# A position-bias table written from 128 partitions in three pieces, and the first loads of inverse blocks issued by ScalarE, in a hybrid DeltaNet and dilated-attention layer

## Chip, cores and metric

One NeuronCore of a Trainium2 chip runs the whole layer. Times are device microseconds of one execution. The reported time of a kernel is the median of several executions; one further execution is taken with a profile, and all rows shown come from that one.

## The reference

One sequence of 2048 tokens with model width 1024, all in float32. Cut to what matters here:

```python
proj = rms_norm(x, norm_w) @ w_in                  # 2048 x 4104
# branch 1: gated delta rule, 4 heads of 128, chunks of 64 tokens
l_mat = a_mat + eye                                # per chunk, lower triangular 64 x 64
u = triangular_solve(l_mat, v * beta);  w = triangular_solve(l_mat, k * beta * exp(gc))
def step(state, (a, q_dec, k_tail, u, w, g_last)): # over the 32 chunks, in order
    v_new = u - w @ state
    o     = q_dec @ state + a @ v_new
    state = state * g_last + k_tail.T @ v_new
y_dn = rms_norm(o) * silu(z)
# branch 2: 8 heads of 64, three dilated windows (128,1), (512,4), (2048,16)
scores = q @ k.T + rel_bias[:, t5_bucket(distance)]   # one bias table per head and pattern
o = softmax-weighted sum of the three patterns, * silu(gate)
out = x + concat(y_dn, o) @ w_out
```

## The kernel before

The work runs in stages, and TensorE is kept filled by mixing a projection (its products go to the PSUM tiles `pj`) with whatever else is due. A scheduler with priorities sets the order of instructions on each engine ahead of time; on the chip each engine runs its list strictly in order.

- **Convolution and inverses** (to about 440 us). The projections of q, k and v of the delta rule are convolved. `stage1a` builds the chunk matrices and stores them to DRAM (`A_d`, `Es_d`); `inverse(hf)` inverts their 32 x 32 diagonal blocks on VectorE and stores them (`A_d`, `D0_d`), first for chunks 0 to 15 (hf 0), then for 16 to 31. Hf 0 is stored at about 370 us and hf 1 at about 440 us.
- **Gate projection** (L187 to L208, `gate_proj`). Its second half, over token blocks 0 and 1, runs from about 444 us, with 24 products a block: TensorE fills a `pj` tile (two of them), VectorE multiplies it into a tile `t` (two of them), ScalarE applies SiLU and issues the store to `gate`.
- **The bias table** (L577 to L590). `rel_bias` (32 x 8) and a one-hot matrix (33 x 768) are loaded into the tile `K` (named `scr` in the code), their product (8 heads x 768 columns) is copied back into `K`, and three transfers write it to DRAM as `bs_d`, each pattern's row of 256 numbers 64 times per head. The attention stage reads the table back with a stride of 255, which gives each query its shifted row. The first such read is at 644 us.
- **Delta rule** (about 450 to 800 us). `stage2(pair, c0)` prepares four chunks of two heads: it loads `kT`, `qT`, `vT`, `Qr`, `E`, `TT` (the inverse blocks, tiles `TTz`) and `D0` (tiles `D0t`), completes the 64 x 64 inverses on TensorE (first step: `A<-D0t,TTz`, L637 before, L642 after) and makes the operands of `chain(pair, c, g)`, the step from chunk to chunk. `dn_out(pair, c0, g)` normalises four chunks, multiplies them by `zs` (loaded there) and stores them to `y_d`. Beside all this the attention's projection (`pj`, 128x256, line L99) fills TensorE.
- **Attention and output projection** (about 800 us to the end).

All loads before the change, and most stores, are issued from SyncE's queue (SP), in order; ScalarE (ACT) issues some stores. Both share eight completion counters, which the tables below call DMAHW0 to DMAHW7 (the number behind the underscore says nothing here). Each transfer takes the next counter, and is issued only when the last transfer that used that counter has landed. So at most eight transfers of the two queues are under way, and an issue can wait for a transfer it has nothing to do with.

Of the kernel before, what the change touches and what calls it, by code (L numbers as in the profile page):

```python
# [8 lines left out]
F32 = mybir.dt.float32  # L9
# [7 lines left out]
P = 128  # L17
S = 2048
# [6 lines left out]
NOSYNC = mybir.DependencyInfo(mybir.DependencyClass.NoSync, mybir.DependencyReason.DATA)  # L25
CH = 64
# [15 lines left out]
N_BUCKETS = 32  # L42
# [38 lines left out]
def dap(t, off, dims):  # L81
    return bass.AP(tensor=t.tensor, offset=t.offset + off, ap=[list(d) for d in dims])


def hybrid(tc, xT, x, norm_w, w_in, conv_w, a_log, dt_bias, dn_norm_w, q_norm_w, k_norm_w,
# [23 lines left out]
    nc = tc.nc  # L109
# [13 lines left out]
    dma = nc.sync.dma_start  # L123
    adma = nc.scalar.dma_start

    dr, _ = pool("dr", space=DRAM)
    qkvT_d = [[dr.tile([P, 32, 2, CH], F32, name=f"cv{w}{p}") for p in range(2)] for w in range(3)]
    zs_d = dr.tile([S, 512], F32, name="zs_d")
    gate_d = [dr.tile([P, S], F32, name=f"gate{p}") for p in range(4)]
    rows_d = dr.tile([4, 4, S], F32, name="rows_d")  # L130
    rstd_d = dr.tile([1, S], F32, name="rstd_d")

    A_d = [dr.tile([2, 16, P, CH], F32, name=f"A{i}") for i in range(2)]
    Es_d = [dr.tile([2, 16, P, CH], F32, name=f"Es{i}") for i in range(2)]
    D0_d = [dr.tile([64, 32, 32], F32, name=f"D0{i}") for i in range(2)]
    qkT_d = [[dr.tile([P, S], F32, name=f"qk{w}{p}") for p in range(4)] for w in range(2)]
    v_d = dr.tile([S, 512], F32, name="v_d")
    y_d = dr.tile([S, 512], F32, name="y_d")
    bs_d = dr.tile([8, 3, 64 * 256], F32, name="bs_d")
    ml_d = [[dr.tile([2, 96, CH], F32, name=f"ml{h}{p}") for p in range(4)] for h in range(2)]  # L140
    F_d = [[dr.tile([3, 2, 1024], F32, name=f"F{h}{p}") for p in range(4)] for h in range(2)]
    mx_d = dr.tile([4, P, S], F32, name="mx_d")
# [76 lines left out]
    nc = engines  # L219
    dma = nc.sync.dma_start  # L220
    adma = nc.scalar.dma_start
# [100 lines left out]
    for kt in range(KT):  # L322
# [14 lines left out]
        for i in range(4):  # L337
            for j, (x_, w_) in enumerate(((xh, 0), (xh, 1), (xl, 0))):
                nc.tensor.matmul(pz[i][:, :260], x_[0][:, kt, i * P:(i + 1) * P], wz[0][kt][w_][:, kt % 4, :260],
                                 start=kt == 0 and j == 0, stop=kt == KT - 1 and j == 2)  # L340
# [3 lines left out]
    n = KT  # L344
# [35 lines left out]
    nc = tc.nc  # L380
    dma = nc.sync.dma_start
    adma = nc.scalar.dma_start
# [12 lines left out]
    at = ba[:, 4:8, :]  # L395
# [180 lines left out]
    scr = at0.tile([P, S], F32, name="K0")  # L576
    rb = scr[:N_BUCKETS + 1, 1536:1544]  # L577
    nc.vector.memset(rb, 1.0)
    dma(scr[:N_BUCKETS, 1536:1544], rel_bias)
    oh = scr[:N_BUCKETS + 1, 768:1536]  # L580
    dma(oh, onehot)
    bv = scr[:8, :768].rearrange("p (a b) -> p a b", a=3)
    for i in range(2):
        pb = psA.tile([P, 512], F32, name="pm", bufs=1)
        n = 512 - 256 * i
        nc.tensor.matmul(pb[:8, :n], rb, oh[:, i * 512:i * 512 + n], start=True, stop=True)
        nc.vector.tensor_copy(scr[:8, i * 512:i * 512 + n], pb[:8, :n])
    for i in range(3):
        dma(dap(bs_d, i * 64 * 256, [[3 * 64 * 256, 8], [256, 64], [1, 256]]),
            bv[:, i, None, :].to_broadcast([8, 64, 256]))  # L590

# [4 lines left out]
    turn2 = [0]  # L598
    SU = psD.tile([P, 4, P], F32, name="SU", bufs=1)

    def stage2(pair, c0):

        hf, cc = divmod(c0, 16)
        u0 = pair * 32 + c0
        m0 = pair * 32 + cc * 2
# [7 lines left out]
        dma(vT, qkvT_d[2][pair][:, c0:c0 + 4])  # L615
        Qr = dn.tile([P, 4, 2, CH], F32, name="Qr", bufs=1)
        for s_ in range(2):
            dma(Qr[:, :, s_], dap(rows_d, (12 + 2 * pair + s_) * S + c0 * CH, [[0, P], [CH, 4], [1, CH]]))
        WQ = dn.tile([P, 4, 2, P], F32, name="WQ", bufs=3)
        for s_ in range(2):  # L620
            nc.gpsimd.tensor_tensor(WQ[:, :, s_, (1 - s_) * CH:(2 - s_) * CH], Qr[:, :, s_], qT[:, :, 1 - s_],
                                    op=ALU.mult)
        E = dn.tile([P, 4, CH], F32, name="E2", bufs=2)
        dma(E, Es_d[hf][pair, cc:cc + 4].rearrange("u p i -> p u i"))
        TT = TTz[n2 % 2]
        D0 = dn.tile([P, 4, 32], F32, name="D0t", bufs=2)
        Xs = dn.tile([P, 4, 32], F32, name="Xs", bufs=1)
        for s_ in range(2):
            a = s_ * CH
            dma(TT[a:a + CH, :, a:a + CH], A_d[hf][pair, cc:cc + 4, a:a + CH].rearrange("u p i -> p u i"))  # L630
            dma(D0[a:a + 32], dap(D0_d[hf], (m0 + s_) * 1024, [[32, 32], [2048, 4], [1, 32]]))
        pa = psD.tile([P, 512], F32, name="A", bufs=2)
        px, pn = pa[:, :256].rearrange("p (a u i) -> p a u i", a=2, u=4), pa[:, 256:260]
        for u in range(4):
            for s_ in range(2):
                a, b = s_ * CH, s_ * CH + 32
                nc.tensor.matmul(px[b:b + 32, 0, u], TT[a:a + 32, u, b:b + 32], D0[a:a + 32, u], start=True, stop=True)  # L637
        for s_ in range(2):
            b = s_ * CH + 32
            nc.vector.tensor_copy(Xs[b:b + 32], px[b:b + 32, 0])  # L640
        for u in range(4):
            for s_ in range(2):  # L642
                a, b = s_ * CH, s_ * CH + 32
                nc.tensor.matmul(px[a:a + 32, 1, u], Xs[b:b + 32, u], TT[b:b + 32, u, b:b + 32], start=True, stop=True)
        for s_ in range(2):
            a = s_ * CH
# [4 lines left out]
        for u in range(4):  # L651
            nc.tensor.matmul(pq[:, u], kT[:, u].rearrange("p s i -> p (s i)"), qT[:, u].rearrange("p s i -> p (s i)"),
                             start=True, stop=True)
        for u in range(4):
            nc.tensor.matmul(pn[:, u:u + 1], q2[:, u], one, start=True, stop=True)
        at_ = dn.tile([P, 4, P], F32, name="at_", bufs=3)
        nc.gpsimd.memset(at_[:CH, :, :CH], 0.0)  # L657
        nc.gpsimd.memset(at_[CH:, :, CH:], 0.0)
        for s_ in range(2):
            a, b = slice(s_ * CH, (s_ + 1) * CH), slice((1 - s_) * CH, (2 - s_) * CH)  # L660
# [6 lines left out]
        Ks = dn.tile([P, 4, 2, P], F32, name="Ks", bufs=3)  # L667
# [27 lines left out]
        U = dn.tile([P, 4, P], F32, name="U", bufs=3)  # L695
        nc.scalar.copy(U, pu)
        o4 = dn.tile([P, 4, P], F32, name="o4", bufs=2)
        return dict(WQ=WQ, at=at_, Ks=Ks, U=U, o4=o4)

    Sst = []  # L700
    mark = {}
# [34 lines left out]
    def dn_out(pair, c0, g):  # L736
        u0 = pair * 32 + c0
        zs = dn.tile([P, 4, P], F32, name="zs", bufs=1)
        for s_ in range(2):
            h = 2 * pair + s_  # L740
            dma(zs[(1 - s_) * CH:(2 - s_) * CH], dap(zs_d, c0 * CH * 512 + h * P, [[512, CH], [CH * 512, 4], [1, P]]))
        f = dn.tile([P, 2, 4], F32, name="f", bufs=2)
        nc.vector.tensor_scalar(f[:, 0], ssqq[:, u0:u0 + 4], EPS, EPS * P, op0=ALU.add, op1=ALU.mult)
        nc.vector.scalar_tensor_tensor(f[:, 1], ssqo[:, u0:u0 + 4], 1.0 / P, f[:, 0], op0=ALU.mult, op1=ALU.add)
        nc.gpsimd.tensor_tensor(f[:, 1], f[:, 1], mhalf[:, :4], op=ALU.pow)
        for u in range(4):
            nc.vector.scalar_tensor_tensor(g["o4"][:, u], g["o4"][:, u], f[:, 1, u:u + 1], zs[:, u],
                                           op0=ALU.mult, op1=ALU.mult)
        for s_ in range(2):
            h = 2 * pair + s_  # L750
            dma(dap(y_d, c0 * CH * 512 + h * P, [[512, CH], [CH * 512, 4], [1, P]]),
                g["o4"][(1 - s_) * CH:(2 - s_) * CH])


    prio = {"chain": 1000000, "prep": PRPREP, "out": PROUT}

    def at_prio(k, f, *args):
        tc.cur_priority = prio[k]
        r = f(*args)
        prio[k] = tc.cur_priority  # L760
        return r

    G = {}
    for p_ in range(2):
        G[p_] = at_prio("prep", stage2, p_, 0)
    for c0 in range(0, 32, 4):
        cur = dict(G)
        for u in range(4):
            for p_ in range(2):
                at_prio("chain", chain, p_, c0 + u, cur[p_])  # L770
            if u == 0:
                for p_ in range(2):
                    if c0 + 4 < 32:
                        G[p_] = at_prio("prep", stage2, p_, c0 + 4)
        for p_ in range(2):
            at_prio("out", dn_out, p_, c0, cur[p_])
    close(psD_g)
    close(dn_g)

# [41 lines left out]
    nc = engines  # L821
# [140 lines left out]
    def heads(hf, p):  # L962
# [5 lines left out]
        def load():  # L968
            g["q1"] = at0.tile([P, 1024], F32, name="q1", bufs=QB)
            g["k1"] = KC[p % 2] if hf else K0[:, p % 2 * 1024:(p % 2 + 1) * 1024]  # L970
            dma(g["q1"], qkT_d[0][p][:, T0:T0 + 1024])
            dma(g["k1"], qkT_d[1][p][:, :1024 * (hf + 1)])
            g["bias"] = bias = at0.tile([P, 3, 192], F32, name="bias", bufs=2)
            for s_ in range(2):
                dma(bias[s_ * CH:(s_ + 1) * CH],
                    dap(bs_d, (2 * p + s_) * 3 * 64 * 256 + 63, [[255, CH], [64 * 256, 3], [1, 192]]))
            g["kc"] = {0: g["k1"].rearrange("p (c i) -> p c i", c=1)}

        def keys(pat):
# [259 lines left out]
    for i, g in enumerate(G):  # L1239
        b = 12 * i  # L1240
# [279 lines left out]
```

## Time and profile before

| | |
|---|---|
| median of three executions | 1446.1 us (1442.88 to 1447.8) |
| profiled execution | 1442.2 us, of which the span from first to last instruction is 1440.4 us |
| TensorE busy | 1374.0 us, 95% of the span |
| VectorE, ScalarE, GpSimd busy | 62%, 47%, 30% |
| mean granted TensorE clock | 0.987 |

TensorE is the engine to watch: it is busy nearly all the time, so what matters is where it stands still and where its clock is low. The granted clock is 1.00 (2.4 GHz) or 0.50 (1.2 GHz).

### The profile page before, as it was taken

To read this page: it belongs to the slowest core of one execution; us is meant where nothing else is said; L and a number is where in the kernel's file an instruction comes from. 1 tells how busy PE (TensorE), PEld (TensorE's weight loads), DVE (VectorE), ACT (ScalarE), POOL (GpSimd) and SP (SyncE) were. 2 spreads that over 40 slices of the span, in tenths; PEclk is the share of its full clock that TensorE was granted. 3 is DMA by queue.
4 is the path that set the end of the run, shared out by engine and by line. 5 is a ranking of instruction groups with operands and counts; after the bars stand their busy time and mean duration, and the time that the engine had idled before them with its cause. 6 is when DMAs were issued, how large, how long until landed. Compare 5 with 4: busy or idle time off the path is not lost.

```text
span 1440.4 us, 28745 instructions
## 1 busy us (share of the span) xinstructions
PE 1374.0 (95%) x10234; PEld 1223.6 (85%) x10234; DVE 897.2 (62%) x2786; ACT 680.1 (47%) x1937; POOL 427.2 (30%) x499
## 2 busy tenths in 40 slices
PE   7999999999998998999999899999998999999988
PEld 7998777777877887999999889999887778888877
DVE  6526678799894365777777554544354645466455
ACT  7634436642221333444444476665555545555520
POOL 0000000000002112442432523657466274655500
PEclk9999999999999999999999999999998999999999
DMA  7653445773557556566554554464448574755764
GB/s 218 165 117 70 99 102 133 156 132 55 116 88 193 147 83 171 133 166 168 133 143 76 124 127 116 100 174 119 112 118 246 146 247 134 216 154 171 200 175 150
DMA packets 301154, 205.00 MB, mean 142 GB/s; under 512 B 149283, under 2 KB 271027, under 8 KB 300500
## 3 DMA queue, kind: packets, MB, share of 16 engines
q1 hardware_dynamic: 233924, 171.70, 48.6%
q10 hardware_dynamic: 67088, 31.47, 7.9%
q8 instruction: 81, 1.33, 0.4%
q14 instruction: 61, 0.50, 0.1%
HBM read 142.61 MB, written 60.50 MB: 141 GB/s over the span
## 4 chain that ended last, share of the span: by engine, by line
PE 61%; DVE 15%; DMA 11%; ACT 5%; issue 4%; POOL 2%; SPq 1%; ACTq 0%; DVEq 0%; POOLq 0%
PE pj L99 13%; PE po L99 8%; PE pz L99 5%; PE sc L99 5%; PE pj L206 4%; PE pj L207 4%; PE pj L208 4%; PE pv L99 3%; PE pt L99 3%; DVE cy L473 3%; DVE inv L540 2%; DMA kT<-cv 2%; PE C L714 2%; PE SU L720 2%; ACT pr L99 2%
## 5 line engine op out<-in xcount | busy, mean ns | idle before, releaser
L99 ACT ACTIVATE pr<-pr,ml 128x192 f32<-128x192 f32 (+2 forms) x384 | 156.8, 410 | 161.6 <-DVE ml L99 161.6
L99 PE MATMUL pj<-wh,xh 128*128 128x256 f32 (+1 forms) x776 | 227.7, 293 | 0.0
L99 PE MATMUL pj<-wl,xh 128*128 128x256 f32 (+1 forms) x776 | 227.6, 293 | 0.0
L99 PE MATMUL pj<-wh,xl 128*128 128x256 f32 (+1 forms) x776 | 225.8, 291 | 0.0
L208 PE MATMUL pj<-xh,wl 128*128 128x512 f32 x512 | 203.9, 398 | 3.6 <-DVE wl L192 3.6
L206 PE MATMUL pj<-xh,wh 128*128 128x512 f32 x512 | 203.9, 398 | 1.3 <-ACT cy L475 1.2
L207 PE MATMUL pj<-xl,wh 128*128 128x512 f32 x512 | 203.2, 397 | 0.0
L99 PEld LDWEIGHTS pj<-wl,xh 128*128 128x128 f32 x776 | 148.3, 191 | 0.6 <-issue 0.4
L99 PEld LDWEIGHTS pj<-wh,xl 128*128 128x128 f32 x776 | 148.3, 191 | 0.0
L99 PEld LDWEIGHTS pj<-wh,xh 128*128 128x128 f32 x776 | 148.1, 191 | 0.2
L99 DVE CUSTOM_DVE_ANT_0 pr<-sc,bias 128x192 f32<-128x192 f32 (+2 forms) x384 | 100.1, 307 | 71.0 <-PE sc L99 70.2
L208 PEld LDWEIGHTS pj<-xh,wl 128*128 128x128 f32 x512 | 96.6, 189 | 27.3 <-DVE wl L192 5.3
L206 PEld LDWEIGHTS pj<-xh,wh 128*128 128x128 f32 x512 | 96.8, 189 | 24.4 <-ACT cy L475 1.6
L473 DVE SCALAR_TENSOR_TENSOR cy<-cu,cw,cy 128x512 f32<-128x512 f32 x144 | 107.9, 752 | 15.2 <-ACT cy L471 13.6
L207 PEld LDWEIGHTS pj<-xl,wh 128*128 128x128 f32 x512 | 96.6, 189 | 21.9
L99 POOL COPY qz<-q 64x512 f32<-64x512 f32 x96 | 92.5, 964 | 57.7 <-PE sc L99 54.7
L657 POOL MEMSET at__4520<- 64x256 f32 x1 | 0.3, 304 | 354.5 <-PE pj L207 354.5
L99 DVE COPY pT<-pt 64x128 f32<-64x128 f32 (+2 forms) x220 | 69.3, 323 | 56.4 <-PE pt L99 53.1
L99 PE MATMUL po<-xh,mhh 128*128 128x512 f32 x212 | 88.8, 419 | 3.9 <-ACT mhh L99 3.9
L99 PE MATMUL pv<-pT,V 128*64 128x128 f32 (+1 forms) x1328 | 79.1, 269 | 9.8 <-DVE pT L99 4.7
L99 PE MATMUL po<-xl,mhh 128*128 128x512 f32 x212 | 88.1, 415 | 0.0
L99 PE MATMUL po<-xh,mhl 128*128 128x512 f32 x212 | 87.7, 414 | 0.3 <-DVE mhl L99 0.3
(360 smaller groups left out, 3151.8 us busy)
## 6 DMA issues: line engine op xcount, KB each, us to landing
wraw<-in_w_in SPq DMA_DIRECT2D x44, 512.0 KB, 6.9
cv<-cy ACTq DMA_DIRECT2D x48, 256.0 KB, 2.7
Fb<-F SPq DMA_DIRECT2D x64, 192.0 KB, 5.7
xr<-in_xT SPq DMA_DIRECT2D x32, 256.0 KB, 4.5
kT<-cv SPq DMA_DIRECT2D x32, 256.0 KB, 3.3
qk<-qs ACTq DMA_DIRECT2D x64, 128.0 KB, 3.3
res<-in_x SPq DMA_DIRECT2D x13, 512.0 KB, 5.2
V<-v_d SPq DMA_DIRECT2D x20, 256.0 KB, 6.2
```

Source lines behind the costliest of these rows:

```text
L99: i = f(*args, **kw)
L206: nc.tensor.matmul(ps, wh[:, k, c * P:(c + 1) * P], xh[tb][:, kt, :], start=kt == 0, stop=False)
L207: nc.tensor.matmul(ps, wh[:, k, c * P:(c + 1) * P], xl[tb][:, kt, :], start=False, stop=False)
L208: nc.tensor.matmul(ps, wl[:, k, c * P:(c + 1) * P], xh[tb][:, kt, :], start=False, stop=kt == KT - 1)
L473: nc.vector.scalar_tensor_tensor(y, u[:, i:i + 512], cw[:, ct, i:i + 1], y, op0=ALU.mult, op1=ALU.add)
L540: nc.vector.tensor_tensor(pr_[:, :i, :i], Tt[:, :i, :i], L[:, None, :i, i].to_broadcast([P, i, i]), op=ALU.mult)
L657: nc.gpsimd.memset(at_[:CH, :, :CH], 0.0)
L714: nc.tensor.matmul(pc[:, s_], g["WQ"][:, u, s_], S0[:, s_], start=True, stop=True)
L720: nc.tensor.matmul(su[:, s_], g["Ks"][:, u, s_], VN, start=True, stop=True)
```

## The change

Three things change.

1. The table's layout in DRAM goes from (head, pattern) to (pattern, head), and its source in SBUF from 8 partitions to 128. For that the bias columns are first repeated 16 times by a VectorE copy (`rb16`, L583 after), and the product has 128 rows instead of 8.
2. The three writes of `bs_d` leave the place behind the product. Each becomes `bias_out(i, after)`, called once behind `dn_out` of chunks 0, 4 and 8, and held behind the load of `zs` there.
3. The first preparation of each pair (`stage2(p_, 0)`) issues its loads of `E`, `TT` and `D0` from ScalarE's queue; and the first two `zs` loads are held behind the last `Qr` load of these preparations.

```diff
-    bs_d = dr.tile([8, 3, 64 * 256], F32, name="bs_d")
+    bs_d = dr.tile([3, 8, 64 * 256], F32, name="bs_d")
...
-    bv = scr[:8, :768].rearrange("p (a b) -> p a b", a=3)
+    rb16 = scr[:N_BUCKETS + 1, 1552:1680]
+    nc.vector.tensor_copy(rb16.rearrange("p (h c) -> p h c", h=8), rb[:, :, None].to_broadcast([N_BUCKETS + 1, 8, 16]))
+    bv = scr[:, :768].rearrange("p (a b) -> p a b", a=3)
...
-        nc.tensor.matmul(pb[:8, :n], rb, oh[:, i * 512:i * 512 + n], start=True, stop=True)
-        nc.vector.tensor_copy(scr[:8, i * 512:i * 512 + n], pb[:8, :n])
-    for i in range(3):
-        dma(dap(bs_d, i * 64 * 256, [[3 * 64 * 256, 8], [256, 64], [1, 256]]),
-            bv[:, i, None, :].to_broadcast([8, 64, 256]))
+        nc.tensor.matmul(pb[:, :n], rb16, oh[:, i * 512:i * 512 + n], start=True, stop=True)
+        nc.vector.tensor_copy(scr[:, i * 512:i * 512 + n], pb[:, :n])
+    def bias_out(i, after):
+        d = dma(dap(bs_d, i * 8 * 64 * 256, [[4 * 256, P], [256, 4], [1, 256]]),
+                bv[:, i, None, :].to_broadcast([P, 4, 256]))
+        tc.add_manual_dep(d.ins, after.ins.name, NOSYNC, reason="behind the loads of a group of chunks")
...
-    def stage2(pair, c0):
+    def stage2(pair, c0, dma2=dma):
...
-        dma(E, Es_d[hf][pair, cc:cc + 4].rearrange("u p i -> p u i"))
+        dma2(E, Es_d[hf][pair, cc:cc + 4].rearrange("u p i -> p u i"))
...
-            dma(TT[a:a + CH, :, a:a + CH], A_d[hf][pair, cc:cc + 4, a:a + CH].rearrange("u p i -> p u i"))
-            dma(D0[a:a + 32], dap(D0_d[hf], (m0 + s_) * 1024, [[32, 32], [2048, 4], [1, 32]]))
+            dma2(TT[a:a + CH, :, a:a + CH], A_d[hf][pair, cc:cc + 4, a:a + CH].rearrange("u p i -> p u i"))
+            dma2(D0[a:a + 32], dap(D0_d[hf], (m0 + s_) * 1024, [[32, 32], [2048, 4], [1, 32]]))
...
+            z = dma(zs[(1 - s_) * CH:(2 - s_) * CH], dap(zs_d, c0 * CH * 512 + h * P, [[512, CH], [CH * 512, 4], [1, P]]))
+            if c0 == 0:
+                tc.add_manual_dep(z.ins, last_D0[0].ins.name, NOSYNC, reason="behind the first preparations'")
...
-        G[p_] = at_prio("prep", stage2, p_, 0)
+        G[p_] = at_prio("prep", stage2, p_, 0, adma)
+    last_D0 = [G[1]["D0"]]
...
-            at_prio("out", dn_out, p_, c0, cur[p_])
+            z = at_prio("out", dn_out, p_, c0, cur[p_])
+        if c0 < 12:
+            at_prio("out", bias_out, c0 // 4, z)
...
-                    dap(bs_d, (2 * p + s_) * 3 * 64 * 256 + 63, [[255, CH], [64 * 256, 3], [1, 192]]))
+                    dap(bs_d, (2 * p + s_) * 64 * 256 + 63, [[255, CH], [8 * 64 * 256, 3], [1, 192]]))
```

(`last_D0` holds the last `Qr` load of pair 1, whatever its name says.)

**Order on ScalarE**, at the start of the delta rule, before. `gate_67` is the last store of the gate projection's first half, and the `t` tiles are the first of its second half:

```order
L488 DMA gate_67<-cy 128x512
L487 ACTIVATE t_4225<-t_4225 128x512
L488 DMA gate_64<-t_4225 128x512
L649 ACTIVATE tmp<-qT 128x512
L487 ACTIVATE t_4254<-t_4254 128x512
L488 DMA gate_64<-t_4254 128x512
```

And now, with the counters that each row waits for:

```order
L629 DMA E_4478<-Es_72 128x4x64 [waits DMAHW5_49]
L635 DMA TTz_4455<-A_70 64x4x64 [waits DMAHW0_49]
L636 DMA D0t<-D_74 32x4x32 [waits DMAHW2_49]
L635 DMA TTz_4455<-A_70 64x4x64 [waits DMAHW4_49]
L636 DMA D0t<-D_74 32x4x32 [waits DMAHW6_49]
L654 ACTIVATE tmp<-qT 128x512 [waits DMAHW7_49]
L629 DMA E_4580<-Es_72 128x4x64 [waits DMAHW0_49]
L635 DMA TTz_4456<-A_70 64x4x64 [waits DMAHW2_49]
L636 DMA D0t<-D_74 32x4x32 [waits DMAHW3_49]
L635 DMA TTz_4456<-A_70 64x4x64 [waits DMAHW4_49]
L636 DMA D0t<-D_74 32x4x32 [waits DMAHW5_49]
L487 ACTIVATE t_4225<-t_4225 128x512 [waits DVE_49]
```

Ten loads and the square of `qT` now stand ahead of the first SiLU of the gate's second half. Counter DMAHW6 was last taken by the load of `kT`, DMAHW7 by `qT`, DMAHW3 and DMAHW5 by the two `Qr` loads, all four on SP, DMAHW4 by the last `wraw` load.

**Order on TensorE** at the same place, before. The `pj` rows are the third block of the gate's second half, and its last row is the one ahead of `A<-D0t`:

```order
L207 MATMUL pj<-xl_139,wh 128x512
L208 MATMUL pj<-xh_138,wl 128x512
L637 MATMUL A<-D0t,TTz_4457 32x32
L652 MATMUL A<-qT,kT 128x128
L637 MATMUL A<-D0t,TTz_4457 32x32 x7
L652 MATMUL A<-qT,kT 128x128 x3
L206 MATMUL pj<-xh_140,wh 128x512
```

And now, with the counters:

```order
L206 MATMUL pj<-xh_138,wh 128x512
L642 MATMUL A<-D0t,TTz_4455 32x32 [waits DMAHW2_49,DMAHW0_49,PE_49]
L657 MATMUL A<-qT,kT 128x128 [waits DMAHW7_49,DMAHW6_49,PE_49]
L657 MATMUL A<-qT,kT 128x128 x3
L642 MATMUL A<-D0t,TTz_4455 32x32 [waits DMAHW6_49,DMAHW4_49]
L642 MATMUL A<-D0t,TTz_4455 32x32 x6
L207 MATMUL pj<-xl_139,wh 128x512
```

The same step stands 14 products of 128x512 earlier: ten of the third block's 24 are ahead of it, and 14 behind.

**Order on SyncE** around the writes of the table, before:

```order
L99 DMA wraw<-in_w_in 128x4x256
L589 DMA bs_d<-K_4444 8x64x256
L630 DMA TTz_4458<-A_70 64x4x64 x2
L631 DMA D0t<-D_74 32x4x32 x2
L589 DMA bs_d<-K_4444 8x64x256 x2
L614 DMA qT<-cv_57 128x512
L624 DMA E_5084<-Es_72 128x4x64
L613 DMA kT<-cv_59 128x512
L615 DMA vT<-cv_62 128x512
```

And now, the first of the three (the other two stand in the same way behind the outputs of chunks 4 and 8):

```order
L629 DMA E_5185<-Es_72 128x4x64
L758 DMA y_d<-o_4567 64x4x128 x2
L746 DMA zs<-zs_d 64x4x128 x2
L593 DMA bs_d<-K_4444 512x1x256
L618 DMA kT<-cv_60 128x512
L620 DMA vT<-cv_61 128x512
```

All three stood within five rows of the queue, ahead of the loads for chunks 8 to 11; now one stands behind each of three groups.

## Rows read from the trace of the kernel before

**Rows 1.** The page, busy time of each engine over the whole span, with instructions.

```profile
PE 1374.0 (95%) x10234; PEld 1223.6 (85%) x10234; DVE 897.2 (62%) x2786; ACT 680.1 (47%) x1937; POOL 427.2 (30%) x499
```

**Rows 2.** What TensorE (PE) waited for between 440 and 700 us: the line that waited, what ended the wait, us in total, times, longest.

```profile
PE A L675 <- DMA vT<-cv: 6.7, 1, 6.7
PE A L637 <- DMA D0t<-D: 3.7, 1, 3.7
PE A L694 <- ACT tmp L685: 1.2, 1, 1.2
```

**Rows 3.** Stretches of the span: from and to, length, busy time of each engine with instructions, granted TensorE clock, busy share of the 16 DMA engines, GB/s.

```profile
463.00:469.70 6.70, 5.19 (x30) 4.39 (x31) 1.42 (x4) 0.67 (x2) 1.40 (x2) 0.50 0.77 194
...
508.00:541.50 33.50, 30.72 (x311) 29.45 (x309) 21.72 (x70) 11.11 (x39) 6.84 (x10) 1.00 0.55 88
541.50:548.00 6.50, 2.53 (x12) 2.56 (x13) 0.00 (x0) 0.00 (x0) 0.21 (x1) 0.50 0.46 123
548.00:561.00 13.00, 11.76 (x120) 11.25 (x120) 8.23 (x26) 5.17 (x15) 6.69 (x10) 0.99 0.82 197
561.00:640.00 79.00, 77.54 (x771) 75.49 (x766) 61.27 (x187) 36.23 (x120) 31.88 (x44) 1.00 0.57 148
```

**Rows 4.** TensorE in order of time around the first stop: start, duration, line, operation; in brackets the idle time ahead of it and what ended it.

```profile
457.21 0.39 PE L206 MATMUL pj<-xh,wh 128*128 128x512 f32 x1
...
460.45 0.40 PE L208 MATMUL pj<-xh,wl 128*128 128x512 f32 x1
464.51 0.28 PE L637 MATMUL A<-D0t,TTz 32*32 32x32 f32 x2 [3.66 <-DMA D0t<-D]
...
467.31 0.77 PE L206 MATMUL pj<-xh,wh 128*128 128x512 f32 x1
...
469.90 0.40 PE L206 MATMUL pj<-xh,wh 128*128 128x512 f32 x1
```

**Rows 5.** TensorE around the second stop.

```profile
538.34 0.39 PE L728 MATMUL C<-VN,at__4622 128*128 128x128 f32 x2
545.47 1.09 PE L675 MATMUL A<-cs,vT 128*128 128x128 f32 x4 [6.74 <-DMA vT<-cv]
...
552.65 1.16 PE L694 MATMUL A<-tmp,TTz 128*128 128x128 f32 x8 [1.24 <-ACT tmp L685]
```

**Rows 6.** SyncE's issues at the start of the delta rule: start, us that the issue took (in all), line, transfer.

```profile
447.16 0.34 SPq L579 DMA_DIRECT2D K<-in_rel_bias  x1
...
448.10 2.48 SPq L741 DMA_DIRECT2D zs<-zs_d  x2
450.78 2.51 SPq L613 DMA_DIRECT2D kT<-cv  x1
...
461.24 0.39 SPq L631 DMA_DIRECT2D D0t<-D  x1
```

**Rows 7.** SyncE's issues around the writes of the table.

```profile
508.05 0.29 SPq L589 DMA_DIRECT2D bs_d<-K  x1
...
519.44 0.81 SPq L589 DMA_DIRECT2D bs_d<-K  x2
...
528.73 4.01 SPq L613 DMA_DIRECT2D kT<-cv  x1
532.83 3.91 SPq L615 DMA_DIRECT2D vT<-cv  x1
```

**Rows 8.** Links of the chain that ended last, between 365 and 560 us: start, us, what. For a transfer it runs from issue to landing.

```profile
445.22 5.55 DMA big<-rstd_d
450.78 10.44 DMA kT<-cv
461.24 3.14 DMA D0t<-D
...
528.73 16.01 DMA kT<-cv
544.82 6.04 DMA qT<-cv
```

**Rows 9.** The DMA engines from 520 to 540 us, in 40 slices of 0.5 us: busy share of the 16 engines in tenths, rounded down, and GB/s.

```profile
DMA  6544444444678444445844544456854444578444
GB/s 125 112 66 49 53 49 51 53 51 49 86 139 193 49 51 53 51 49 71 154 60 51 82 49 49 49 61 123 203 80 49 49 49 49 70 111 215 72 49 49
```

**Rows 10.** Transfers by kind, with KB each and median us from issue to landing: one of the stretch 560 to 700 us, then one of 444 to 462 us.

```profile
wraw<-in_w_in SPq DMA_DIRECT2D x5, 512.0 KB, 6.5
...
K<-in_rel_bias SPq DMA_DIRECT2D x1, 1.0 KB, 6.1
```

**Rows 11.** ScalarE (ACT) and VectorE (DVE) in order of time, three rows and two; brackets as in Rows 4.

```profile
450.79 0.63 ACT L487 ACTIVATE t<-t 128x512 f32<-128x512 f32 x1 [5.07 <-DVE t L486]
...
461.89 0.63 ACT L649 ACTIVATE tmp<-qT 128x512 f32<-128x512 f32 x1 [10.47 <-DMA qT<-cv]
...
551.29 0.27 ACT L729 COPY o<-C 128x128 f32<-128x128 f32 x1 [14.02 <-DMA qk<-qs]
...
450.06 0.69 DVE L486 TENSOR_TENSOR t<-pj,big 128x512 f32<-128x512 f32 x1 [2.97 <-DMA big<-rstd_d]
...
461.13 0.69 DVE L486 TENSOR_TENSOR t<-pj,big 128x512 f32<-128x512 f32 x1 [5.12 <-DMA gate<-t]
```

More of the change, by code (lines that the diff above doesn't have):

```diff
@@ L617, in stage2 @@
         for s_ in range(2):
-            dma(Qr[:, :, s_], dap(rows_d, (12 + 2 * pair + s_) * S + c0 * CH, [[0, P], [CH, 4], [1, CH]]))
+            d0 = dma(Qr[:, :, s_], dap(rows_d, (12 + 2 * pair + s_) * S + c0 * CH, [[0, P], [CH, 4], [1, CH]]))
         WQ = dn.tile([P, 4, 2, P], F32, name="WQ", bufs=3)
@@ L697, in stage2 @@
         o4 = dn.tile([P, 4, P], F32, name="o4", bufs=2)
-        return dict(WQ=WQ, at=at_, Ks=Ks, U=U, o4=o4)
+        return dict(WQ=WQ, at=at_, Ks=Ks, U=U, o4=o4, D0=d0)
     Sst = []
@@ L740, in dn_out @@
             h = 2 * pair + s_
-            dma(zs[(1 - s_) * CH:(2 - s_) * CH], dap(zs_d, c0 * CH * 512 + h * P, [[512, CH], [CH * 512, 4], [1, P]]))
+            z = dma(zs[(1 - s_) * CH:(2 - s_) * CH], dap(zs_d, c0 * CH * 512 + h * P, [[512, CH], [CH * 512, 4], [1, P]]))
+            if c0 == 0:
+                tc.add_manual_dep(z.ins, last_D0[0].ins.name, NOSYNC, reason="behind the first preparations'")
         f = dn.tile([P, 2, 4], F32, name="f", bufs=2)
@@ L752, in dn_out @@
                 g["o4"][(1 - s_) * CH:(2 - s_) * CH])
+        return z
     prio = {"chain": 1000000, "prep": PRPREP, "out": PROUT}
@@ L763, in hybrid @@
     G = {}
+    last_D0 = []
     for p_ in range(2):
-        G[p_] = at_prio("prep", stage2, p_, 0)
+        G[p_] = at_prio("prep", stage2, p_, 0, adma)
+    last_D0 = [G[1]["D0"]]
     for c0 in range(0, 32, 4):
```

## The prediction

> **What bounds the kernel now.** The page comes first: TensorE is busy 95% of the span [rows 1], so a change is worth what it takes from TensorE's idle time and from its time at the lower clock. Next, the list of what TensorE waited for in the stretch that the change touches: two waits stand out, 6.7 us for a load of `vT` and 3.7 us for one of `D0t`, then 1.2 us for a ScalarE result [rows 2]. The stretches say how much there is in all: from 508 to 561 us TensorE is busy 30.72 + 2.53 + 11.76 = 45.01 of 53 us, so 7.99 us are idle, while from 561 to 640 us, where the same delta-rule steps run on, it idles 1.46 of 79 us. And behind each stop the clock is granted at 0.50 (1.2 GHz) for some 6.5 us, 463.0 to 469.7 and 541.5 to 548.0, and 1.00 before and after [rows 3]. Work in such a stretch takes twice its time.
>
> The two stops have different causes. **The second** (538.7 to 545.5) [rows 5]: SP issues the three table writes at 508.05 and 519.44; behind them single issues take 4 us, and a `kT` load issued at 528.73 [rows 7] lands 16.01 us later, a `qT` load behind it in 6.04 [rows 8]. The slices show why: wherever only the writes are under way, between 4 and 5 tenths of the engines' time are busy and 49 to 53 GB/s move [rows 9], which is half the engines. One write of 524 KB takes 524 / 51 = 10.3 us at that rate, three take 31, which from 508 ends at 539. ScalarE is caught as well: it stands 14.02 us, ended by a store of its own queue [rows 11], since the queues share the completion counters; its next work is late for TensorE at 552.65 by 1.24 us [rows 5].
>
> **The first** (460.85 to 464.51) [rows 4]: the first `D0t` is issued at 461.24 [rows 6], just as `kT` lands (450.78 + 10.44 = 461.22), and takes 3.14 us [rows 8]. It waits its turn in SP's list and for the counter that `kT` used.
>
> **What the change is worth, second stop.** The writes leave this place, so the 6.74 us and the 1.24 us behind go [rows 5], and with them the lower clock: 2.53 us of work at 0.50 [rows 3] would take 1.27. Sum: 6.74 + 1.24 + 1.27 = 9.25 us. What is late next there? The loads that stood behind the writes. Free of them, SP would issue the late `vT` (532.83 [rows 7]) some 10 us earlier, ahead of TensorE's need at 538.7, and the stretch behind shows this pace to hold (1.46 us idle in 79).
>
> The writes themselves come back one at a time behind `zs` of chunks 0, 4 and 8, between about 540 and 630 us. From 128 partitions each can use 16 engines. No row shows this write. Bounds: at the rate per engine that it has now it takes half of 10.3, 5.1 us; below, nothing at all. Nearest is a `wraw` load of the same 512 KB, which lands in 6.5 us; five of them run between 560 and 700 us [rows 10] while TensorE idles 1.46 us up to 640. I take nothing for the three, covered as those loads are; without that cover each costs up to 5.1 us of late loads.
>
> **First stop.** This part is not what it seems. The `D0t` step stands 14 products earlier in TensorE's list. The step from the 457.21 row to the 460.45 row is 14 products, so one takes 0.231 us, and TensorE now reaches the step at 460.85 - 14 x 0.231 = 457.6. And the loads, though on ScalarE's queue, still wait for counters: the second `D0t` for the one that `kT` holds (DMAHW6), the `kT` x `qT` products for those two loads. So the question is when `kT` lands. Its own counter comes free with the first `big` load, by 450.06 [rows 11] instead of 450.78, and `zs` is no longer ahead of it (256 KB, at the 194 GB/s of the stretch behind [rows 3] 1.3 us). With its 10.44 us kept, `kT` lands at 460.5; with the `zs` share off, at 459.2. Middle 459.9. Then 3.14 us for `D0t` [rows 8]: TensorE goes on at about 463.1, after 457.6, with only the four `kT` x `qT` products between. Seven small products later, 463.6, it resumes with 14 `pj` products that before were already done. Before, the product at 469.90 is the seventh behind the step [rows 4], so six were done by then. Now the same point comes after 20 products: 463.6 + 20 x 0.231 = 468.2 at full clock, 1.7 us sooner. But a stop this long lowered the clock both times [rows 3]. If it falls again, from about 460 for as long as before (6.7 us), half of the time from 463.1 to 466.7 is lost, 1.8 us, and the point is where it was. I take 0. Bounds: if `kT` takes only the 5.55 us of `big`, the nearest load of its size [rows 8], it lands at 455.6, `D0t` at 458.8, the stop is 1.2 us and the clock stays: 463.6 - 458.8 - 0.5 = 4.3 us sooner than the middle case, and 1.7 more for that case at full clock: 6.0 us gained. If `kT` lands no sooner than now, at 461.2, all is 1.3 us later than in the middle case at the lower clock: up to 1.3 us lost.
>
> **Small parts, at nothing.** The new VectorE copy of the bias columns stands ahead of the first product with `big` and waits for `rel_bias`, issued at 447.16 [rows 6] and landing 6.1 us later [rows 10], at 453.3. That product moves from 450.06 [rows 11] to about 453.5; the third `pj` block, which starts 10 products before 457.5, at 455.1, needs its tile back only then. Cover 0.9 us; beyond it TensorE stops earlier, in time that it would lose at 457.6 anyway. ScalarE's ten issues hold its SiLU of `t` from 450.79 [rows 11] to about 464: the last of them wait for the counters of the two `Qr` loads, which SP issues some 4 us behind `kT`, at 454, and which land at 464 if they take the 10.44 us of `kT`. The store of the first `t`, behind two SiLUs of 0.63 us, is then issued at 465.3 and lands at 470.9 with the 5.55 us of `big` (the same 256 KB). VectorE's third product waits for that tile, as it did at 461.13 [rows 11], and frees its PSUM tile 0.7 us later, at 471.6. The third block ends at 463.6 + 14 x 0.231 = 466.8 at the earliest, the fourth uses the other tile for 24 x 0.231 = 5.5 us, and the fifth needs this one at 472.3. Cover 0.7 us; a store that takes longer costs TensorE what is beyond. The product of 128 rows instead of 8 has the same 512 columns.
>
> **Sum.** 9.25 + 0 + 0 = 9.25 us: 1442.2 - 9.3 = 1432.9 for an execution like the profiled one. That one is 3.9 us below the median of the three; I carry the difference to the median, 1446.1 - 9.3 = 1436.8. All behind 561 us is released by instructions, so it moves forward as a block.
>
> **Rivals.** *Both stops go* (chance 0.18): `kT` lands early, 1446.1 - 9.3 - 6.0 = 1430.8. For it: transfers of this size landed in 5.55 us five microseconds before. Against: `kT` stands behind the same two `wraw` loads.
>
> *The first stop gets worse* (0.14): ScalarE's loads only take share from `kT`, which lands no sooner, while TensorE's list expects it earlier: 1.3 us back, 1438.1. For it: the DMA engines are 0.77 busy even after the worst [rows 3]. The Trainium skill, "DMA: Bandwidth & Descriptors", section "Issuing engines are not separate DMA queues", says that transfers from any issuing engine run on the same 16 DMA engines and that a second issuer saves issue time only; by that rule this rival would be the likeliest for this part. The trace neither shows nor excludes it: no load here is issued from ScalarE.
>
> *The gain is spread, not removed* (0.10): the packets stay as slow and each write, 10.3 us as now, costs a third of the 9.25: no change, 1446.1. For it: each piece repeats one SBUF row to DRAM as before. Against: the source is then confined to few engines no longer.
>
> *Slower* (0.06): the writes now lie ahead of loads with little slack. Now three in a row cost 9.25 us in 31, because loads had been issued well ahead. If each still holds SP's loads for 10.3 us and a load has only the 4 us that it needs to land to spare, each stops TensorE for 6.3 us: 18.9 against 9.25, 1455.8. It decides from a stop of 3.1 us per write.
>
> **Numbers.** The forecast has 0.52. A measurement of this kernel tells about 0.3%, 4.3 us, from no change. Faster by that are the forecast and the first two rivals: 0.84; same 0.10; slower 0.06. The range reaches from the early case, 1430.8, less the scatter of a median, to the worse first stop, 1438.1, plus the 3.9 us between the profiled execution and the median: 1430 to 1442; outside lie the last two rivals, 0.16.
>
> **What would show it.** Right: the wait for `vT` is gone from TensorE's list, the granted clock is 1.00 from 500 to 560 us, a table write shows a busy share near 1 instead of half, and no wait over 2 us takes its place up to 640. For the first stop: the wait for `D0t` starts at about 457.6 and ends near 463, with a stretch at 0.50 behind. Wrong: a wait on a load behind any of the three writes, or a ScalarE stop over 5 us at 450 to 470 that TensorE meets.

## The result, and the profile after

The changed kernel takes 1437.4 us in the median of 13 runs (1433.2 to 1442.6), beside 1445.4 us of the kernel before on the same chip (13 runs): ratio 0.995, 95% interval 0.9933 to 0.9968. A second series gave 1434.0 beside 1443.4 us, ratio 0.9932 (0.9909 to 0.9955). The forecast was 1436.8 us, within 1430 to 1442. The total came out as forecast; one step on the way did not, and the first stop, which the change left as it was, turned out to be removable by another edit.

TensorE's work is the same, and its share of the span is one point higher than in [rows 1]. The page after:

```profile
PE 1372.9 (96%) x10234; PEld 1223.3 (85%) x10234; DVE 904.9 (63%) x2787; ACT 680.4 (47%) x1937; POOL 426.7 (30%) x499
```

What TensorE waited for between 440 and 700 us, as in [rows 2]:

```profile
PE A L642 <- DMA D0t<-D: 3.5, 1, 3.5
PE C L719 <- DVE o L737: 2.8, 1, 2.8
PE pj L206 <- DVE t L486: 0.6, 1, 0.6
```

The 6.7 us for `vT` and the 1.2 us behind it are gone, the first stop has its old size, and 2.8 us for the tile `o` are new. The same stretches as in [rows 3] (length, busy time of PE, PEld, DVE, ACT, POOL, granted clock, DMA share, GB/s):

```profile
508.00:541.50 33.50, 33.50 (x331) 32.08 (x331) 24.86 (x78) 13.50 (x47) 10.66 (x17) 1.00 0.41 110
541.50:548.00 6.50, 6.50 (x70) 6.34 (x69) 5.82 (x17) 2.13 (x7) 3.13 (x4) 1.00 0.77 184
548.00:561.00 13.00, 13.00 (x128) 12.84 (x127) 9.32 (x26) 6.83 (x21) 1.83 (x2) 1.00 0.65 165
561.00:640.00 79.00, 76.23 (x736) 74.44 (x735) 58.53 (x183) 34.44 (x114) 31.98 (x43) 0.98 0.60 157
```

From 508 to 561 TensorE has no idle time left, and the 6.5 us at half clock run at full clock. From 561 to 640 it idles 2.77 us instead of 1.46, at a clock of 0.98 instead of 1.00. The first stop, in order of time as in [rows 4]:

```profile
456.05 0.50 PE L206 MATMUL pj<-xh,wh 128*128 128x512 f32 x1 [0.58 <-DVE t L486]
...
458.25 0.40 PE L206 MATMUL pj<-xh,wh 128*128 128x512 f32 x1
462.15 0.22 PE L642 MATMUL A<-D0t,TTz 32*32 32x32 f32 x2 [3.51 <-DMA D0t<-D]
...
464.54 0.63 PE L208 MATMUL pj<-xh,wl 128*128 128x512 f32 x1
464.96 0.63 PE L206 MATMUL pj<-xh,wh 128*128 128x512 f32 x1
...
469.98 0.39 PE L206 MATMUL pj<-xh,wh 128*128 128x512 f32 x1
```

It begins 2.2 us earlier than before, ends 2.4 us earlier, and products of 512 columns then follow each other in 0.42 us, the half clock, instead of 0.23; the product that stood at 469.90 in [rows 4] starts at 469.98. What ends this stop, in the chain that ended last, is the first `D0t` load:

```profile
454.55 7.46 DMA D0t<-D
```

ScalarE issues it at 454.55, behind a `TTz` load whose counter came free when a `wraw` load landed at 453.81, and it lands at 462.01, 2 us behind `kT` (460.10). The new stop comes 90 us behind the second one. The chain of what released what, in order of time:

```profile
624.77 0.52 SPq L758
625.35 5.33 DMA y_d<-o
630.78 0.27 ACT o L734
631.08 0.29 DVE o L737
...
631.81 0.68 PE C L719 x4
```

A group's output tile (`o4`, printed as `o`) has two buffers, one per pair of heads. The first copy of the next group into it (ScalarE, L734) waits until the store of the last group has landed, VectorE's step waits for that copy, and TensorE for VectorE: 2.77 us. SP's issues ahead of that store:

```profile
616.34 0.61 SPq L593 DMA_DIRECT2D bs_d<-K  x1
...
619.38 0.62 SPq L99 DMA_DIRECT2D wraw<-in_w_in  x1
620.09 2.60 SPq L635 DMA_DIRECT2D TTz<-A  x2
622.78 3.18 SPq L758 DMA_DIRECT2D y_d<-o  x2
```

The third table write is among them. A smaller stop of the same kind, 1.81 us, follows at 744.81. The writes themselves have become short. The first one, 536 to 544 us in 40 slices of 0.2 us, and its row among the transfers (KB, us to landing):

```profile
DMA  1008999998359548999999999899897999999898
...
bs_d<-K SPq DMA_DIRECT2D x1, 512.0 KB, 5.4
```

It is issued at 537.96, in the tenth slice; from the sixteenth on, a microsecond later, nearly the whole time of the 16 engines is busy where [rows 9] showed half of it, and the write lands in 5.4 us beside other loads. The third landed in 3.9 us.

### The profile page after: what moved, and what is told of

Same layout as the page of the kernel before. It is cut to its first block, busy times and chain, and to the rows that moved or that the text cites. A ratio compares the mean times of both kernels' runs of the same rounds, so it can differ in the third digit from the quotient of the medians.

```text
span 1436.0 us, 28743 instructions
## 1 busy us (share of the span) xinstructions
PE 1372.9 (96%) x10234; PEld 1223.3 (85%) x10234; DVE 904.9 (63%) x2787; ACT 680.4 (47%) x1937; POOL 426.7 (30%) x499
## 4 chain that ended last, share of the span: by engine, by line
PE 64%; DVE 15%; DMA 10%; ACT 5%; issue 4%; POOL 2%; SPq 0%; ACTq 0%; DVEq 0%; POOLq 0%
PE pj L99 14%; PE po L99 9%; PE sc L99 6%; PE pz L99 5%; PE pj L206 4%; PE pj L207 4%; PE pj L208 4%; PE pv L99 4%; PE pt L99 3%; DVE cy L473 3%; DVE inv L540 2%; PE C L719 2%; ACT pr L99 2%; PE SU L725 2%; DMA V<-v_d 2%
## 5 line engine op out<-in xcount | busy, mean ns | idle before, releaser
L99 POOL TENSOR_TENSOR Fb<-Fb,op 128x256 f32<-128x256 f32 x84 | 70.5, 853 | 64.9 <-DMA Fb<-F 51.5
```

The lines of the kernel that those rows point to most:

```text
L99: i = f(*args, **kw)
```

## The experiments

Most runs are read against one table, worked out from the traces: how much earlier (minus) the k-th product of TensorE starts than the k-th product before, with the difference that the execution had already brought along at 440 us (up to 3.9 us) taken off. The columns are the times of that product in the kernel before. Where the order differs, small and large products are mixed differently, which shifts a value by some microseconds; at 822 us all delta-rule steps are done in every kernel.

| kernel | 530 | 561 | 644 | 822 | ratio to before (95%) |
|---|---|---|---|---|---|
| changed | 0.1 | -10.0 | -7.0 | -6.2 | 0.995 (0.9933 to 0.9968) |
| changed, again | 0.7 | -9.4 | -3.3 | -5.5 | 0.9932 (0.9909 to 0.9955) |
| e1 table alone | 1.7 | -8.1 | -8.8 | -5.6 | 0.9934 (0.9918 to 0.995) |
| e2 loads alone | 0.2 | -0.2 | 0.5 | 0.2 | 1.000 (0.9989 to 1.0012) |
| e3 128 partitions, old place | 1.9 | -8.0 | -9.4 | -2.6 | 0.9988 (0.9975 to 1.0002) |
| e4 8 partitions, three places | 0.4 | -9.4 | 11.3 | 11.7 | 1.008 (1.006 to 1.0099) |
| e5 changed, third `o4` | 0.9 | -9.2 | -10.8 | -12.7 | 0.989 (0.9868 to 0.9911) |
| e6 as e1, 48 products more | 0.1 | -9.7 | -10.6 | -9.7 | 0.9921 (0.9899 to 0.9944) |
| e7 as e1, weights later | -4.1 | -13.9 | -14.9 | -10.9 | 0.9903 (0.9878 to 0.9928) |
| e8 before, weights later | -6.0 | -6.8 | -7.7 | -5.2 | 0.9959 (0.9936 to 0.9982) |
| e9 e5, weights later | 3.2 | -6.9 | -8.5 | -11.9 | 0.9899 (0.9865 to 0.9933) |
| e10 as e9, 48 products more | 4.3 | -5.8 | -7.3 | -10.9 | 0.9904 (0.9874 to 0.9935) |
| e11 as e7, 48 products more | -4.6 | -14.4 | -15.1 | -14.9 | 0.989 (0.9859 to 0.9922) |

Behind 822 us two executions of the changed kernel drift apart (-6.4 and -11.8 at 1355 us), so a single profile says nothing on differences there.

### One part at a time: e1 and e2

e1 is the changed kernel without its third part:

```diff
-        G[p_] = at_prio("prep", stage2, p_, 0, adma)
+        G[p_] = at_prio("prep", stage2, p_, 0)
...
-            if c0 == 0:
-                tc.add_manual_dep(z.ins, last_D0[0].ins.name, NOSYNC, reason="behind the first preparations'")
```

> The changed kernel with the first preparations' loads back on SyncE and the first zs loads not held; the table is written from 128 partitions in three places. Theory (all of the gain comes from the table): about the changed kernel's 1437 us; the wait for D0t of 3.7 us at 461 us and the low clock behind it are back where they were, the wait for vT is gone. Rival (the loads on ScalarE's queue save something of their own): 1439 us or more, and a first stop that costs over 2 us more than in the changed kernel.

Measured: 1432.3 us, ratio 0.9934. TensorE has one wait left between 440 and 700 us:

```profile
PE A L642 <- DMA D0t<-D: 4.2, 1, 4.2
```

e2 is the kernel before with that third part alone (the writes as before).

> The kernel before with the first preparations' loads on ScalarE's queue and the first zs loads held; the table as before, from 8 partitions in one place. Theory: no change, 1445 us, with the 6.7 us wait for vT near 540 us still there and the wait for D0t moved to 458 to 462 us. Rival (the loads alone bring something): 1441 us or less.

Measured: 1442.9 us, ratio 1.000. Its three longest waits are the two of [rows 2] and one for the tile `o`, as in the changed kernel but shorter:

```profile
PE A L675 <- DMA vT<-cv: 6.3, 1, 6.3
PE A L637 <- DMA D0t<-D: 4.0, 1, 4.0
PE C L714 <- DVE o L732: 1.3, 1, 1.3
```

This last wait ends at 641.2, behind a `y_d` store that takes 6.46 us, with the table's writes still at their old place.

The whole gain is the table's, and the loads through ScalarE's queue are worth nothing, to 0.12%. This is also what the Trainium skill says ("DMA: Bandwidth & Descriptors", section "Issuing engines are not separate DMA queues"): a second issuing engine saves only the time of issuing; the run agrees.

e1 has the third write at the same place in SP's list and no stop at 630 us. Its lead, 8.8 us at 644, shrinks to 5.6 at 822. The place is one wait of 4.80 us ahead of the TensorE step at 783.08; in the chain it is the same thing:

```profile
774.96 6.76 DMA y_d<-o
...
781.79 0.28 ACT o L734
...
783.08 0.98 PE C L719 x3
```

### Partitions and place: e3 and e4

e3 writes from 128 partitions, but all three at the old place; e4 from 8 partitions, at the three new places. Both without the third part.

```diff
 e3
+    for i in range(3):
+        bias_out(i, None)
...
-        if c0 < 12:
-            at_prio("out", bias_out, c0 // 4, z)
```

```diff
 e4
-        d = dma(dap(bs_d, i * 8 * 64 * 256, [[4 * 256, P], [256, 4], [1, 256]]),
-                bv[:, i, None, :].to_broadcast([P, 4, 256]))
+        d = dma(dap(bs_d, i * 8 * 64 * 256, [[64 * 256, 8], [256, 64], [1, 256]]),
+                bv[:, i, None, :].to_broadcast([8, 64, 256]))
```

> The kernel before with the table's source on 128 partitions, the three writes still one behind another in the old place (SP list near 508 us); loads as before. If the number of engines was the cause: each write lands in under 7 us, the wait for vT near 540 us is gone, and the third write is not near 616 us, so the new 2.8 us wait near 630 us of the changed kernel is gone too: 1435 us. If the place was the cause: SP's loads behind them are still late and 3 to 7 us of the second stop remain: 1440 to 1443 us.

> The kernel before with the table still written from 8 partitions at half the engines, but in three places behind chunks 0, 4 and 8 as in the changed kernel; loads as before. If the number of engines was the cause: each write holds the engines 10 us and costs TensorE about 3 us, three of them about as much as the one stop before: 1445 us. If the place was the cause: about 1437 us as the changed kernel, with waits near 630 us no longer than its 2.8 us.

Both lose the second stop: e3 leads by 8.0 us and e4 by 9.4 us at 561. Neither keeps this lead. In e4, whose writes are issued at 542, 589 and 634, TensorE stops four more times, up to 564, 606, 642 and 654 us. Its waits from 440 to 700 us, what ScalarE waited longest for between 540 and 665 us, and the DMA engines from 596 to 612 us in slices of 0.4 us:

```profile
PE A L658 <- ACT TTz L650: 6.4, 2, 4.7
PE A L640 <- DMA D0t<-D: 4.0, 1, 4.0
PE A L655 <- ACT U L699: 3.2, 1, 3.2
PE C L717 <- DVE o L735: 2.0, 1, 2.0
```

```profile
ACT o L732 <- DMA y_d<-o: 25.8, 4, 10.3
```

```profile
DMA  4444444585444598846997498446799997220000
GB/s 51 51 51 51 51 51 51 74 145 90 60 67 151 190 220 186 186 89 124 179 216 151 110 328 284 117 86 115 189 331 344 360 350 267 89 56 0 0 0 0
```

The writes move 51 GB/s through less than half of the engines' time, as in [rows 9]. From 561 to 644 us the kernel loses 9.4 + 11.3 = 20.7 us, twice what the three writes in a row cost; 11.6 of it are these stops (6.4 + 3.2 + 2.0), and the granted clock is 0.89 on average from 555 to 660 us. Three of the four stops (up to 564, 606 and 654 us) stand behind ScalarE's copy into `o`, which waits for the last group's store: the wait of the changed kernel's new stop, and not one for a load. Whether a third `o4` buffer would take most of this price away was not tried. So the three places without the 128 partitions make the kernel slower: 1452.9 us, where 1445 was expected.

e3 is harder: 1441.1 us, ratio 0.9988, not clear of no change, although its writes land in 4.0 us (median) and TensorE is busy without a gap from 508 to 640. The 1435 us expected for this cause were missed, and the time lies in the rival's range, but not for the rival's reason, since the second stop is gone:

```profile
508.00:561.00 53.00, 53.00 (x508) 50.07 (x507) 38.55 (x113) 21.09 (x70) 17.24 (x23) 1.00 0.60 153
561.00:640.00 79.00, 79.00 (x774) 77.22 (x773) 58.84 (x181) 34.65 (x112) 31.38 (x42) 1.00 0.55 144
```

The lead of 9.4 us at 644 is 2.6 at 822. Two waits take most of it, 2.2 us for `VN` at 660 and 4.2 us at 744, and behind the latter stands again a transfer of a group's output, this time the `zs` load that SP issues behind the store of the last group:

```profile
736.16 5.47 DMA zs<-zs_d
...
743.66 0.34 DVE WQ L698
...
744.14 1.84 PE C L721 x8
```

VectorE stands at the multiplication with `zs` while TensorE's operand `WQ` waits in its list. e3 and e1 differ in the writes' place alone, but with it the scheduler's order; that the order, and not the place as such, decides which wait is met is argued, not shown. In time, then, neither half of the table's change pays by itself; the 0.7% of e1 needs both.

### The new stop: e5

```diff
-        o4 = dn.tile([P, 4, P], F32, name="o4", bufs=2)
+        o4 = dn.tile([P, 4, P], F32, name="o4", bufs=3)
```

The list of instructions is the same on every engine; only the wait for the buffer goes.

> The changed kernel once more, beside the next three on one chip. Expected: 1437 us, ratio 0.995, the wait for the o tile near 630 us again (about 2.8 us), the last product of the chain near 793 us of a span of 1436.

> The changed kernel with a third buffer for o4 (the tile that a group's outputs are gathered in and stored from); the order of instructions is the same on every engine. Theory: the new stop at 629 to 632 us is a wait for an o4 buffer, whose store stands behind the third table write on SP's queue; with a third buffer the 2.8 us wait and the half clock behind it are gone, TensorE is busy 79.0 of the 79 us from 561 to 640 (76.2 before), and the chain is some 3 us earlier at 640. What of that is left at the end depends on the products held back until the delta rule is done: ratio 0.993 if all stays, 0.995 if the end gives it back. Rival: the stop is the order's (the chain's operands come late whatever the buffer): wait and ratio as in the changed kernel, 0.995.

The changed kernel, run beside it, took 1434.0 us, e5 1428.8, and their runs do not overlap (1430.9 to 1439.0 against 1426.1 to 1430.0). Two fences of the changed kernel, the stretch from 561 to 640 and TensorE's step behind the stop, and then the same two with the third buffer:

```profile
561.00:640.00 79.00, 74.72 (x716) 72.93 (x715) 57.29 (x175) 33.15 (x107) 31.18 (x42) 0.97 0.57 151
```

```profile
634.36 0.87 PE L719 MATMUL C<-S,WQ 128*128 128x128 f32 x4 [4.28 <-DVE o L737]
```

```profile
561.00:640.00 79.00, 78.22 (x766) 76.21 (x764) 59.87 (x185) 35.93 (x116) 31.60 (x43) 1.00 0.58 153
```

```profile
640.21 0.68 PE L719 MATMUL C<-S,WQ 128*128 128x128 f32 x4 [0.50 <-DVE o L737]
```

The 4.28 us become 0.50, the lead at 644 grows from 3.3 to 10.8 us, and the third buffer is worth 5.2 us in the median, more than expected. The rival (the operands come late whatever the buffer) falls. The buffer also takes most of the smaller waits of this kind away. What ScalarE's copy into `o` waited for the store between 440 and 830 us, before the change, in the changed kernel (first series) and with the third buffer (us in total, times, longest):

```profile
ACT o L729 <- DMA y_d<-o: 8.8, 5, 4.4
...
ACT o L734 <- DMA y_d<-o: 26.8, 6, 9.4
...
ACT o L734 <- DMA y_d<-o: 1.9, 1, 1.9
```

What makes the store late is open. The third write alone does not: e1 has it and no stop near 630, and in e2, which has no write there, ScalarE waits 21.0 us in all and TensorE stops for 1.3. A TensorE that is ahead does not either: e2 has no lead, and in e3, which leads by 9.4 us at 644, ScalarE waits 4.1 us. The `wraw` load issued between the third write and the store took 10.3 us where such loads before the change took 6.5 in the median [rows 10].

### The end of the delta rule: e6, e10 and e11

The attention's projection fills TensorE beside the delta rule; its 960th product is held behind the last delta-rule step. These runs let 1008 through:

```diff
-HOLD = 5
+HOLD = 5.25
```

> The table alone (as e1), with 1008 instead of 960 of the later projection's products let in ahead of the delta rule's last step; the order moves only in the last 30 us of the delta rule. Theory: the gain of the removed stop is given back at the end of the delta rule because the products that may fill TensorE are used up sooner (idle from 770 to 800: 7.6 us in e1, 3.1 before the change). 48 products of 0.235 us are 11 us: the idle time falls to about 3 us or under, the chain's last step stays within 4 us of e1's 793, and the time falls by 4 to 5 us below e1: 1428, ratio 0.990. Rival: the end of the delta rule is what all later work waits for, so that products put ahead of it only delay it: chain 3 us later, time of e1 or 3 us over it, ratio 0.9935 to 0.996.

e6 is e1 with this edit. Its idle time from 770 to 800 us fell from the 7.57 us of e1 (the first of the two fences, 30 us less busy time) to 4.09 (the second), its lead at 822 rose from 5.6 to 9.7 us, and the median is 1433.3 us, ratio 0.9921: not to be told from e1.

```profile
770.00:800.00 30.00, 22.43 (x157) 20.92 (x156) 18.87 (x64) 7.87 (x31) 7.42 (x10) 0.89 0.35 62
```

```profile
770.00:800.00 30.00, 25.91 (x195) 24.35 (x194) 18.17 (x63) 9.33 (x30) 7.50 (x10) 0.94 0.40 80
```

> As the run before (third o4 buffer, weights behind the first loads), with 1008 instead of 960 of the later projection's products ahead of the delta rule's last step. If the end of the delta rule lacks products: 2 to 4 us under the run before, ratio 0.983. If not: the same time within 2 us, and the last step of the chain 5 us later with 48 more products done.

> The table alone, weights behind the first loads (as the run that gave 0.9903), with 1008 products instead of 960. There TensorE was idle 6.6 us from 770 to 800, 4.7 of it in one wait with few products left. If lacking products are the cause: idle 3 us or under, 3 us less, ratio 0.988; if the extra products only stand ahead of the chain, 0.990 to 0.992.

Where the third `o4` buffer is there, the extra products give nothing (e10 0.9904, e9 0.9899). Without it, e11 leads by 14.9 us at 822, e7 by 10.9; the times, 0.989 and 0.9903, are too close to tell. My theory that products run out was too simple: in e1 the 4.8 us were the store of `o`, and more products merely cover such a wait (in e6 ScalarE still waits 6.2 us for that store, TensorE 1.9).

### The first stop: e7, e8 and e9

The first load of the projection's weights (`wraw`, 512 KB, converted from 475 us on) is issued at 447.59 in the kernel before, ahead of all the delta rule's loads. e7 (on e1), e8 (on the kernel before) and e9 (on e5) hold it behind the last `Qr` load of the first preparations:

```diff
-            dma(raw[:, :, :256], dap(w_in, ...
+            m = dma(raw[:, :, :256], dap(w_in, ...
...
+            if i == 0 and not held:
+                tc.add_manual_dep(m.ins, last_D0[0].ins.name, NOSYNC, reason="behind the first preparations")
+                held.append(m)
```

> The table alone (as e1), with the first load of weights for the later projection (512 KB) issued behind the first group's loads instead of ahead of them; no other engine's order moves. Theory: the first stop is set by the landing of the first kT, which shares the DMA engines with what was issued ahead of it: without these 512 KB (at the 188 to 194 GB/s of the stretch 2.7 us) kT lands up to 2.7 us sooner and the first stop falls from 4.2 to between 1.5 and 3 us; the time falls by 1 to 2 us, ratio 0.992 to 0.993. Rival: the loads wait for counters or for the inverse's own stores and not for bandwidth: stop and ratio as in e1 (4.2 us, 0.9934); or the weights now come late and TensorE waits for them near 480, 2 us or more.

> The kernel before with one edit: the first load of weights for the later projection is issued behind the first group's loads. No other engine's order moves; the table writes are as before. Theory: that load, not SP's share of the inverse's loads, makes the first stop: the 3.7 us wait for D0t and the half clock behind it go, the first step of the delta rule is 5 to 6 us earlier (SU number 0 at 488, before 493), the second stop (6.7 us) stays or grows a little since TensorE comes to it sooner while the table writes still end near 539 if they start no earlier. Time: 4 to 6 us less if the second stop moves along, ratio 0.996 to 0.997; 1.00 if the second stop only begins sooner and ends when it did. Rival: the first stop comes back from another load.

> The changed kernel with both: the third o4 buffer and the weights behind the first loads. If the two gains are independent: the first stop is gone (5 to 6 us) beside the stop at 630 (5 us in the run with the third buffer): ratio 0.989 less 0.004, 0.985, 1422. If the end of the delta rule takes the gain of the first stop back, as with the table alone: 0.987 to 0.989, with 6 us or more idle from 765 to 795.

In e7 and e8 only SP's list changes. The stop is gone in both; the stretch around it in e8, where the kernel before was busy 9.34 of the 13 us at a clock of 0.74:

```profile
457.00:470.00 13.00, 13.00 (x90) 10.26 (x89) 3.41 (x7) 4.23 (x10) 2.96 (x4) 1.00 0.89 200
```

`kT` lands in 6.0 us there, and in 5.9 us in e7, instead of 10.44 [rows 8]: some 4.5 us sooner, where I gave the 512 KB 2.7 us. Its row in e7 (445 to 470 us):

```profile
kT<-cv SPq DMA_DIRECT2D x2, 256.0 KB, 5.9
```

e8 takes 1437.5 us, ratio 0.9959, with the second stop unchanged (6.9 us for `vT`). So the first stop was worth 5 to 6 us, and one load's place made it.

In e9 the two gains do not add: 1428.8 us, as e5. The first stop is gone, but the weights are now late, and TensorE stops 5.6 us at 481.49:

```profile
470.22 8.66 DMA wraw<-in_w_in
...
480.05 1.23 DVE wl L99
481.49 0.55 PE A L693
```

The conversion of the weights stands ahead of the delta rule's work in VectorE's list, so its wait is everybody's. With the loads on SP's queue (e7, e8, e11) that wait does not appear, and e11, the table alone with the weights behind, gives 1427.3 us. e5, e7, e9, e10 and e11 all beat the kernel before and have lower medians than the changed kernel, but only e5's runs lie wholly below those of the changed kernel taken beside it. Among the five the runs don't decide.

## Why the prediction was right, point by point

**Second stop, 9.25 us: right.** The lead between the products at 530 and 561 us is 10.1 us in both profiles of the changed kernel, against 6.74 + 1.24 + 1.27. The cause of the stop was as named: e3 shows that the writes' speed alone removes it, e4 that spreading alone only puts others in its place.

**The writes at nothing: half right.** The writes land in about the time of the bound (5.4 and 3.9 us, against 5.1), and from 508 to 640 us TensorE waits for no load. But "no wait over 2 us takes its place up to 640" failed: 2.8 and 4.3 us in the two profiles. I had looked for late loads only; what was late was a store, whose landing frees a buffer.

**"All behind 561 us is released by instructions, so it moves forward as a block": wrong.** This is the step that failed. The delta rule's steps are also released by transfers (a group's `y_d` store, its `zs` load), which are queued on SP and take 3 to 7 us where TensorE stops behind them; which of them come late changes with the order. Of 10.0 us at 561, 6.2 were left at 822 in the changed kernel, 5.6 of 8.1 in e1, 2.6 of 8.0 in e3; with the third buffer 9.2 became 12.7. The total still fitted, since the medians gained 8.0 and 9.4 us. The second stop gave 0.85 us more than forecast; how 6.2 and 5.5 us at 822 become such medians is not shown, since the profiles drift apart behind it. So that the total fits is luck, not working.

**First stop at 0: right in size, by another link.** Stop from 457.6, `kT` at 459.9, TensorE on at 463.1, half clock up to 466.7, the old point unmoved: measured 458.6, 460.1 (9.5 us behind its issue), 462.15, 466.7 and 0.08 us. The second `D0t`, which waits for the counter of `kT`, landed at 463.03, as worked out; but what let TensorE go on was the first one, which the prediction took to be there in time and which took 7.46 us from 454.55 to 462.01. The two came within 1.1 us of each other, so the size held partly by luck. e2 says the same in time. The bound of 6.0 us, for a `kT` that lands in 5.55, is what e7 and e8 reached by another edit.

**Small parts: right in kind.** VectorE's copy waited for `rel_bias` until 454.40, and the 0.58 us that it cost TensorE fell into time that the stop took anyway. The store of the first `t` landed at 470.7 (forecast 470.9), and TensorE did not wait for its tile.

**The rivals.** "The gain is spread, not removed" did not come: the packets go through all engines. "Slower" was priced at 1455.8 us, 9.7 more than before, for writes that hold loads for 10.3 us each; e4, the nearest case, took 1452.9, 10.3 more than the kernel before beside it, but mostly through late stores of `o` instead of late loads. "Both stops go" had the right reason against it, the `wraw` loads ahead of `kT`: with one of them moved behind, the stop went.

## What to carry to other kernels

When a stop is removed, don't move all that follows forward as a block: list what behind it is released by a transfer, stores that free a buffer among them, and look how long before TensorE's need each one lands. Count the buffers of a tile that is stored from: a third one was worth 5.2 us here. A large load that nobody needs for 25 us, issued ahead of the smaller ones that are needed next, cost 5 to 6 us here, and a second issuing queue won none of it back. A write of 512 KB from 8 partitions was a slow one (51 GB/s), and in three places it cost twice what it did in one.

## What the hardware showed that I had not expected

- The 512 KB ahead of `kT` cost it some 4.5 us (10.44 against 5.9 and 6.0), where 512 KB at the 194 GB/s of the stretch would take 2.7.
- Three writes that kept the DMA engines half busy cost 9 us in a row and some 20 us when 45 us apart, most of the stops by way of a store that freed a buffer late.
- Moving the first loads to another queue lengthened waits far behind them: ScalarE's for `y_d` stores, from 440 to 830 us, went from 8.8 to 21.0 us in e2, at no cost in the total.
- Executions part early even where they run the same instructions: e3's profiled one was 2.6 us behind at 72 us, long before its edit. A lead has to be read from a point just ahead of the change.
